# The first head pair's q and k loaded into both partition halves, and the buffers of the gated branch in another order

## The chip, the cores and the metric

The kernel runs on one core of a Trainium2 chip. The metric is the device time of one execution in microseconds (us). Before the change the median of three runs is 1768.68 us (1766.93 to 1769.41).

## The reference, cut to what matters

One step of a hybrid layer for 1024 prompt tokens and 64 decode tokens, model width 1024. One projection `h @ w_in` gives q, k, v (512 columns each, 8 heads of 64), the SSM input u and two gates of 1024 columns. Then:

```
z = (q @ k.T) / 8; log_keep = log_sigmoid(-z) where key < query
w = exp(log_sigmoid(z) + sum of log_keep over later visible keys); o_attn = w @ v
o_ssm = y * sigmoid(y @ w_glu)            # y = gelu of the S5 scan's output
merged = sigmoid(g_attn) * (o_attn @ w_branch_attn) + sigmoid(g_ssm) * (o_ssm @ w_branch_ssm)
```

After that come the output projection, a SwiGLU feed-forward layer and the per-layer embedding gate, all with RMS norms. Decode queries attend to a cache of 2048 past rows as well. The raw k and v are outputs too.

## The kernel before, in words

**Arithmetic.** All matrices are float32. For the weight products each operand is split into a rounded high part and the remainder (`split`, L124: ScalarE rounds, VectorE subtracts), and `mm3` (L133) makes three matmuls of one product: high by high, high by low, low by high. A feature-major product (`fm_iter`, L257) takes 128 output columns and goes over the 1088 tokens in three chunks of 364, 362 and 362 (`CH`); with 8 k-tiles a chunk is 24 matmuls into one PSUM bank of tag `pj`, followed by an evacuation `evac`.

**Attention operands.** For scores of a head, one matmul contracts over 128 partitions that hold q's high part in 64 of them and its low part in the other 64. The key tile `ks` holds in `[:, 0]` the high part of k in both halves and in `[:, 1]` the low part in both halves; two matmuls (L764) then give all four products. `project_pair(j)` (L621) prepares two heads. For pairs 1 to 3 it computes q, k, v from weights, chunk by chunk. For pair 0 the three column blocks were computed earlier (`rest`, L1490) and lie in the DRAM scratch `pp`; `projected` (L693) loads them. In both cases q is split into `qh` and `ql` (L633, L634), and four DMAs (L649) copy the halves into the two `qs` tiles; k is split into `kh` and `kl` (L660, L663) and eight DMAs (L677) copy them into the two `ks` tiles. The four tiles qh, ql, kh, kl share the tag `hl` with two buffers. `tok_out` (L698) transposes k and v by TensorE for the outputs; for v it also fills the `vs` tiles by GpSimd.

**The stage before attention.** `glu` (L585) loads y, splits it into `ya`, makes four sigmoid products into `sg`, multiplies by y (L605), splits the result into four `bs` tiles, and then runs eight products `w_branch_ssm` (the "branch stage"): for each m a gate tile `gl` (two buffers) is loaded from `gd` (L613), three chunks of 12 matmuls are multiplied into it (L616), and it is stored again (L618).

**What sets the order.** A queue of dense work (`rest`) holds gate columns; `fill(1)` takes its next piece. `attention` (L861) prepares pair 0, then takes `G3 = 4` pieces of the queue while `self.cut` is 0, when a piece is a whole chunk of 24 matmuls. After that it walks through the string `ORDER`, made by `order` (L52): a digit is a step of that head, `d` a decode step, `p` a step of the projections of pairs 1 to 3, `g` one piece of the queue, `E` an early load for the merge. There `CUT = 3`, and a piece is a third of a chunk. `gs` is how many `g` fall on each of the four pairs. `hold` (L151) keeps p and g pieces behind a recent score matmul. What is left of the queue is taken after attention (`fill(48)`, L1553). The framework orders every engine's instructions by a timeline that it simulates when the program is built, with program order as priority, so instructions of later code can stand before those of earlier code. All loads and stores here are issued by SyncE's queue (SP), in order.

**Memory.** Buffers of a pool get addresses by tag in the order in which tags first appear. `glu` is a left pool; attention has a left pool (`attA`) that begins at the same address, and a right pool (`att`) that grows down from the top, whose first tag is `ks` (three tiles). A tile waits for the earlier tiles whose bytes it reuses (`reuse_waits="tile"`).

Of the kernel before, what the change touches and what calls it, by code (L numbers as in the profile page):

```python
# [8 lines left out]
F32 = mybir.dt.float32  # L9
F32R = mybir.dt.float32r  # L10
BF = mybir.dt.bfloat16
AF = mybir.ActivationFunctionType
OP = mybir.AluOpType
# [4 lines left out]
SEQ = 1024  # L18
DEC = 64
TOK = SEQ + DEC  # L20
PAST = 2048
HD = 64
# [7 lines left out]
CHU = ((0, 368), (368, 360), (728, 360))  # L30
LVL = 3
G1, G2 = 5, 4
G3 = 4
CUT = 3
NC = 3
HP = 5
# [15 lines left out]
def order(L, steps, d0, d1, p0, p1, gs, e):  # L52

    ev = []
    for x in range(8):
        ev += [(x + L * f, 0, str(x)) for f in steps]
    for j in range(4):
        ev += [(2 * j + d0 + (d1 - d0) * k / 5, 1, "d") for k in range(5)]
        if j < 3:
            ev += [(2 * j + p0 + (p1 - p0) * k / (9 * NC), 2, "p") for k in range(9 * NC + 1)]  # L60
        ev += [(2 * j + 2 * (k + .5) / gs[j], 3, "g") for k in range(gs[j])]
    ev.append((e, 4, "E"))
    return "".join(x[2] for x in sorted(ev))


ORDER = order(L=1.7, steps=(0, 0.23, 0.42, 0.76), d0=-0.09, d1=1.77, p0=-0.36, p1=1.49, gs=(9, 15, 3, 21), e=7)


class Net:
# [515 lines left out]
    def glu(self, P):  # L585

        nc = self.nc
        Y, YA, B = [None] * 4, [None] * 4, []
        for k in (0, 2, 1, 3):
            y = P.tile([128, T, NCH], F32, name="y", tag="y", bufs=4)  # L590
            nc.sync.dma_start(y, self.ydr[k * 128:(k + 1) * 128])
            ya = P.tile([128, 2, TOK], F32R, name="ya", tag="ya", bufs=4)
            for c0, n0, n in ((0, 0, SEQ // T), (SEQ, S0, DEC // T)):
                h, l = (ya[:, i, c0:c0 + n * T].rearrange("p (c t) -> p t c", t=T) for i in range(2))
                self.split(h, l, y[:, :, n0:n0 + n])
            Y[k], YA[k] = y, ya
        for m in range(4):
            s = P.tile([128, TOK], F32, name="sg", tag="sg", bufs=2)

            def evac(ci, c0, n, ps, s=s):  # L600
                nc.scalar.activation(s[:, c0:c0 + n], ps, AF.Sigmoid)
            self.fm_cols(self.I["w_glu"][0], m * 128, 4, evac, acts=YA)
            for c0, n0, n in ((0, 0, SEQ // T), (SEQ, S0, DEC // T)):
                v = s[:, c0:c0 + n * T].rearrange("p (c t) -> p t c", t=T)
                nc.vector.tensor_mul(v, v, Y[m][:, :, n0:n0 + n])  # L605
            if "o_ssm" in self.dbg:
                nc.sync.dma_start(self.dbg["o_ssm"][m * 128:(m + 1) * 128], s)
            b = P.tile([128, 2, TOK], F32R, name="bs", tag="bs", bufs=4)
            self.split(b[:, 0], b[:, 1], s)
            B.append(b)  # L610
        for m in range(8):
            g = P.tile([128, TOK], F32, name="gl", tag="gl", bufs=2)
            nc.sync.dma_start(g, self.gd[8 + m])  # L613

            def evac(ci, c0, n, ps, g=g):
                nc.vector.tensor_mul(g[:, c0:c0 + n], ps, g[:, c0:c0 + n])  # L616
            self.fm_cols(self.I["w_branch_ssm"][0], m * 128, 4, evac, acts=B)
            nc.sync.dma_start(self.gd[8 + m], g)  # L618


    def project_pair(self, PB, PA, j, out):  # L621

        nc, P = self.nc, PA
        PJ = PB if j % 2 else PA
        w_in = self.I["w_in"][0]
        qh = P.tile([128, SEQ], F32R, "qh", "hl")
        ql = P.tile([128, SEQ], F32R, "ql", "hl")
        qb = PJ.tile([128, 128], F32, "qb", f"qb{j % 2}")
        nc.gpsimd.memset(qb, 0.0)

        def evac_q(ci, c0, n, ps):
            m = min(n, SEQ - c0)
            nc.scalar.activation(qh[:, c0:c0 + m], ps[:, :m], AF.Copy, scale=0.125)  # L633
            nc.vector.scalar_tensor_tensor(ql[:, c0:c0 + m], ps[:, :m], 0.125, qh[:, c0:c0 + m],  # L634
                                           op0=OP.mult, op1=OP.subtract)
            if m < n:
                for h in range(2):
                    hs = slice(h * 64, (h + 1) * 64)
                    nc.scalar.activation(qb[hs, hs], ps[hs, m:n], AF.Copy, scale=0.125)
        if j:  # L640
            yield from self.fm_iter(w_in, j * 128, 8, evac_q)
        else:
            x = self.projected(PB.tile([128, 2, SEQ], F32R, "ks", "ks").bitcast(F32).rearrange("p a b -> p (a b)")[:, :TOK], 0)
            for ci, (c0, n) in enumerate(CH):
                evac_q(ci, c0, n, x[:, c0:c0 + n])
        Q = [PJ.tile([128, SEQ], F32R, "qs", f"qs{j % 2}") for h in range(2)]
        for h in range(2):
            for i in range(2):
                nc.sync.dma_start(Q[h][i * 64:(i + 1) * 64].bitcast(F32),  # L649
                                  (qh, ql)[i][h * 64:(h + 1) * 64].bitcast(F32))  # L650
        kt = P.tile([128, TOK], F32, "kT", "raw")
        if not j:
            self.projected(kt, 1)
        kn = PJ.tile([128, DEC], F32, "kn", f"kn{j % 2}")
        kh = P.tile([128, SEQ], F32R, "kh", "hl")
        kl = P.tile([128, SEQ], F32R, "kl", "hl")

        def evac_k(ci, c0, n, ps):
            m = min(n, SEQ - c0)
            nc.scalar.activation(kh[:, c0:c0 + m], ps[:, :m], AF.Copy)  # L660
            if j:
                nc.scalar.activation(kt[:, c0:c0 + n], ps, AF.Copy)
            nc.vector.tensor_sub(kl[:, c0:c0 + m], ps[:, :m], kh[:, c0:c0 + m])  # L663
            if m < n:
                nc.vector.tensor_copy(kn, ps[:, m:n])
        if j:
            yield from self.fm_iter(w_in, SBW + j * 128, 8, evac_k)
        else:
            for ci, (c0, n) in enumerate(CH):
                evac_k(ci, c0, n, kt[:, c0:c0 + n])  # L670
        self.tok_out(P, kt, 2, 6, j, None)
        K = []
        for h in range(2):
            ks = PB.tile([128, 2, SEQ], F32R, "ks", "ks")
            for i in range(2):
                for r in range(2):
                    nc.sync.dma_start(ks[i * 64:(i + 1) * 64, r].bitcast(F32),  # L677
                                      (kh, kl)[r][h * 64:(h + 1) * 64].bitcast(F32))
            K.append(ks)
        vt = P.tile([128, TOK], F32, "vT", "raw")  # L680

        def evac_v(ci, c0, n, ps):
            nc.scalar.activation(vt[:, c0:c0 + n], ps, AF.Copy)
        if j:
            yield from self.fm_iter(w_in, 2 * SBW + j * 128, 8, evac_v)
        else:
            self.projected(vt, 2)
        V = [PJ.tile([128, 8, 2, HD], F32R, "vs", f"vs{j % 2}") for _ in range(2)]
        vn = PJ.tile([DEC, 128], F32, "vn", f"vn{j % 2}")
        self.tok_out(P, vt, 3, 7, j, (V, vn))  # L690
        out[j] = list(zip(Q, K, V)), (kn, qb, vn)

    def projected(self, x, i):  # L693
# [167 lines left out]
    def attention(self, P, PA, fill, early):  # L861

        self.oad = [self.dram.tile([128, TOK], F32, name=f"oad{j}") for j in range(4)]
        ops, self.miles = {}, []
        pa = PA.__enter__()
        for _ in self.project_pair(P, pa, 0, ops):
            pass
        self.cut = 0
        for _ in range(G3):
            fill(1)  # L870
        def projections():
            for j in range(1, 4):
                yield from self.project_pair(P, pa, j, ops)
                yield

        def decodes():
            for j in range(4):
                yield from self.decode(P, j, *ops[j][1])

        live = {"p": projections(), "d": decodes()}  # L880
        self.cut = CUT
        for c in ORDER:
            if c == "E":
                PA.__exit__(None, None, None)
                early()
            elif c == "g":
                with self.hold(HG):
                    fill(1)
            elif c == "p":
                with self.hold(HP):  # L890
                    next(live[c], None)
            else:
                if c not in live:
                    j, h = divmod(int(c), 2)
                    live[c] = self.head(P, j, h, *ops[j][0][h])
                next(live[c], None)
        for c in "01234567d":
            for _ in live[c]:
                pass
        self.cut = 0  # L900
# [710 lines left out]
```

## Time and profile before

| | |
|---|---|
| median of three runs | 1768.68 us |
| the profiled execution | 1768.44 us, span from first to last instruction 1766.7 us |
| TensorE busy | 1692.9 us (96%) |
| VectorE, ScalarE, GpSimd busy | 1041.0 (59%), 731.2 (41%), 522.3 (30%) us |
| mean granted TensorE clock | 0.985 of full |

Rows of `windows` views give, for a stretch, its length, the busy time of TensorE, its weight loads, VectorE, ScalarE and GpSimd, each with its number of instructions, then the granted clock (1.00 is 2.4 GHz, 0.50 is 1.2 GHz), the mean busy share of the DMA engines and GB/s. Rows of a `timeline` give start, duration, engine, line, operation, output<-input; brackets hold the idle time before it and what ended it. Rows of groups end with busy time, mean ns of one, idle time before.

### The profile page before, as it was taken

How to read it: one execution, taken by the hardware profiler on the slowest of the kernel's cores; microseconds unless marked ns; L12 is line 12 of the kernel's file. 1: busy time of each engine (PE TensorE's matmuls, PEld its weight loads, DVE VectorE, ACT ScalarE, POOL GpSimd, SP SyncE). 2: the span in 40 equal slices, each digit the busy share in tenths (PEclk: the TensorE clock that was granted, in tenths of full speed). 3: DMA queues.
4: the chain of work that ended last, by engine and by line, in shares of the span. 5: the costliest groups of instructions: out<-in, count | busy, mean ns of one | idle time of the engine just before them, and what ended most of it. 6: DMA issues, size and time to landing. Idle time of an engine off the chain costs nothing.

```text
span 1766.7 us, 24728 instructions
## 1 busy us (share of the span) xinstructions
PE 1692.9 (96%) x9092; PEld 1478.4 (84%) x9092; DVE 1041.0 (59%) x1579; ACT 731.2 (41%) x1355; POOL 522.3 (30%) x450
## 2 busy tenths in 40 slices
PE   8999999989999888899997999999999999999998
PEld 6999999989898877798786788888888877888886
DVE  7437917337768777866464656555555455445674
ACT  6431135135545556533343333333333344444542
POOL 2026200022313233233330544446444213001453
PEclk9999999999999999999998999999999999999999
DMA  8352563874344332157445354445444386665332
GB/s 287 93 148 64 125 148 116 260 187 121 87 107 105 90 98 84 48 174 231 138 154 182 124 154 127 153 138 184 154 139 141 113 303 203 203 190 168 104 111 89
DMA packets 220841, 258.23 MB, mean 146 GB/s; under 512 B 26272, under 2 KB 168720, under 8 KB 220704
## 3 DMA queue, kind: packets, MB, share of 16 engines
q1 hardware_dynamic: 220064, 255.21, 47.8%
q0 software_dynamic: 656, 1.44, 0.6%
q8 instruction: 72, 1.18, 0.3%
q14 instruction: 49, 0.40, 0.1%
HBM read 165.32 MB, written 76.51 MB: 137 GB/s over the span
## 4 chain that ended last, share of the span: by engine, by line
PE 72%; DVE 13%; DMA 6%; ACT 3%; issue 3%; POOL 1%; SPq 1%; DVEq 0%; POOLq 0%; ACTq 0%
PE pj L1205 13%; PE tr L1205 6%; PE pj L137 6%; PE pj L139 6%; PE pj L138 6%; PE z L1371 3%; DVE p L735 3%; PE z L1205 3%; PE pj L1371 3%; PE tr L1371 2%; PE av L811 2%; PE z L138 2%; PE z L139 2%; PE z L137 2%; PE tr L781 1%
## 5 line engine op out<-in xcount | busy, mean ns | idle before, releaser
L137 PE MATMUL pj<-H,wh 128*128 128x362 f32 (+3 forms) x648 | 218.1, 337 | 5.9 <-DVE ql L634 3.7
L139 PE MATMUL pj<-H,wl 128*128 128x362 f32 (+3 forms) x648 | 215.4, 333 | 0.6 <-DVE wl L115 0.6
L138 PE MATMUL pj<-H,wh 128*128 128x362 f32 (+3 forms) x648 | 214.7, 332 | 0.0
L126 DVE TENSOR_TENSOR wl<-raw,wh 128x1024 fp32r<-128x1024 f32 x96 | 131.4, 1373 | 114.0 <-ACT wh L125 112.7
L737 POOL TENSOR_TENSOR w<-w,p 128x383 f32<-128x383 f32 (+4 forms) x68 | 92.7, 1373 | 314.4 <-DVE w L739 185.7
L125 ACT ACTIVATE wh<-raw 128x1024 fp32r<-128x1024 f32 x96 | 101.2, 1059 | 118.3 <-PE z L1371 45.5
L137 PEld LDWEIGHTS pj<-H,wh 128*128 128x128 f32 x648 | 123.0, 190 | 7.6 <-DVE ql L634 4.0
L139 PEld LDWEIGHTS pj<-H,wl 128*128 128x128 f32 x648 | 122.7, 189 | 1.5 <-DVE wl L115 1.0
L138 PEld LDWEIGHTS pj<-H,wh 128*128 128x128 f32 x648 | 123.0, 190 | 1.0 <-issue 0.4
L1205 PE MATMUL pj<-H,s 128*128 128x512 f32 x480 | 118.2, 395 | 0.0
L148 POOL TENSOR_TENSOR rs<-rs,mhalf 128x1 f32<-128x1 f32 (+1 forms) x54 | 32.6, 605 | 277.6 <-DVE rs L147 277.5
L1205 PEld LDWEIGHTS pj<-H,s 128*128 128x128 f32 x480 | 89.9, 188 | 21.0 <-DVE c L1238 0.3
L125 ACT ACTIVATE s<-st 128x512 fp32r<-128x512 f32 x80 | 50.3, 629 | 124.3 <-PE pj L1205 112.8
L1139 POOL TENSOR_TENSOR st<-raw 128x512 f32<-128x512 f32 x40 | 60.9, 1524 | 132.3 <-DVE H L126 54.0
L126 DVE TENSOR_TENSOR s<-st,s 128x512 fp32r<-128x512 f32 x80 | 68.1, 852 | 39.2 <-ACT s L125 38.5
L119 ACT ACTIVATE wh<-raw 128x1024 fp32r<-128x1024 f32 (+1 forms) x52 | 46.6, 898 | 99.7 <-PE av L138 52.1
L115 DVE TENSOR_TENSOR wl<-raw,wh 128x1024 fp32r<-128x1024 f32 (+1 forms) x50 | 51.1, 1022 | 57.7 <-ACT wh L119 57.6
L786 DVE TENSOR_TENSOR wtl<-tr,wth 128x512 fp32r<-128x512 f32 (+2 forms) x112 | 55.2, 496 | 50.5 <-ACT wth L785 50.0
L785 ACT ACTIVATE wth<-tr 128x512 fp32r<-128x512 f32 (+2 forms) x112 | 50.3, 453 | 83.3 <-PE tr L781 42.1
L733 ACT ACTIVATE p<-z 128x512 f32<-128x512 f32 (+4 forms) x116 | 59.0, 509 | 42.6 <-PE z L835 16.7
L735 DVE TENSOR_TENSOR_SCAN p<-p,zero 128x384 f32<-128x384 f32 (+4 forms) x68 | 73.9, 1094 | 0.2
L1205 PE MATMUL pj<-H,wh 128*128 128x512 f32 x224 | 72.5, 401 | 0.6 <-ACT H L125 0.4
(553 smaller groups left out, 4634.0 us busy)
## 6 DMA issues: line engine op xcount, KB each, us to landing
sd<-c SPq DMA_DIRECT2D x77, 256.0 KB, 3.2
raw<-sd SPq DMA_DIRECT2D x77, 256.0 KB, 2.8
raw<-in_w_in_dram SPq DMA_DIRECT2D x32, 512.0 KB, 5.5
raw<-in_w_ffn_gate_dram SPq DMA_DIRECT2D x22, 512.0 KB, 3.7
raw<-in_w_ffn_up_dram SPq DMA_DIRECT2D x22, 512.0 KB, 4.7
wd<-in_w_ffn_down_dram SPq DMA_DIRECT2D x44, 256.0 KB, 3.4
td<-wd SPq DMA_DIRECT2D x22, 512.0 KB, 3.2
raw<-td SPq DMA_DIRECT2D x44, 256.0 KB, 3.0
```

What stands on the lines that cost most here:

```text
L125: self.nc.scalar.activation(wh, raw, AF.Copy)
L126: self.nc.vector.tensor_sub(wl, raw, wh)
L137: self.nc.tensor.matmul(out, wh, xh, start=i == 0, stop=False)
L138: self.nc.tensor.matmul(out, wh, xl, start=False, stop=False)
L139: self.nc.tensor.matmul(out, wl, xh, start=False, stop=i == n - 1)
L733: nc.scalar.activation(p, z, AF.Sigmoid, scale=-1.0)
L735: nc.vector.tensor_tensor_scan(p[:, ::-1], p[:, ::-1], self.zero.to_broadcast([128, n]), 1.0 if carry is None else carry, op0=OP.mult, op1 ...
L737: (nc.gpsimd if e == 'g' else nc.vector).tensor_tensor(w[:, :n - 1], w[:, :n - 1], p[:, 1:], op=OP.mult)
L786: nc.vector.tensor_sub(wl[:, a:b], ps[:, a:b], wh[:, a:b])
L1139: op(t, x, y)
L1205: self.nc.tensor.matmul(out, a[i][:, k], b[j][:, k], start=start and k == i == j == 0, stop=stop and k == 3 and i == 1, skip_group_check=n ...
L1371: nc.tensor.matmul(B[b + n], x[:, 0, c], y[:, 1], start=new and p == j == 0, stop=p == 10 and j == 2, skip_group_check=not new)
```

## The change

For pair 0 a new function `first_pair` replaces `project_pair`. It loads each head's 64 rows of q twice, into both halves of the partitions, and of k likewise, straight into the final tiles. ScalarE rounds all 128 rows of q; VectorE overwrites the second half with the remainder. k is split in place. The staging tiles of tag `hl` and the twelve copies between SBUF tiles are not used for pair 0. In `glu` the tiles `ya`, `bs` and the first two `gl` are allocated ahead of `y` and `sg`. `G3` goes from 4 to 0 and `gs[0]` from 9 to 13.

```diff
-G3 = 4
+G3 = 0
-ORDER = order(L=1.7, ..., gs=(9, 15, 3, 21), e=7)
+ORDER = order(L=1.7, ..., gs=(13, 15, 3, 21), e=7)
 def glu(self, P):
-        Y, YA, B = [None] * 4, [None] * 4, []
+        Y = [None] * 4
+        YA, B = ([P.tile([128, 2, TOK], F32R, name=n, tag=n, bufs=4) for _ in range(4)] for n in ("ya", "bs"))
+        GL = [P.tile([128, TOK], F32, name="gl", tag="gl", bufs=2) for m in range(2)]
...
-            g = P.tile([128, TOK], F32, name="gl", tag="gl", bufs=2)
+            g = GL[m] if m < 2 else P.tile([128, TOK], F32, name="gl", tag="gl", bufs=2)
...
+    def first_pair(self, PB, PA, out):
+        nc = self.nc
+        Q = [PA.tile([128, SEQ], F32R, "qs", "qs0") for h in range(2)]
+        x = PB.tile([128, 2, SEQ], F32R, "ks", "ks").bitcast(F32)
+        K = [PB.tile([128, 2, SEQ], F32R, "ks", "ks") for h in range(2)]
...
+        for h in range(2):
+            rows = slice(h * 64, h * 64 + 64)
+            for i in range(2):
+                nc.sync.dma_start(x[i * 64:i * 64 + 64, h], self.pp[0][rows, :SEQ])
+            for i in range(2):
+                nc.sync.dma_start(K[h][i * 64:i * 64 + 64, 1].bitcast(F32), self.pp[1][rows, :SEQ])
+            nc.scalar.activation(Q[h], x[:, h], AF.Copy, scale=0.125)
+            nc.vector.scalar_tensor_tensor(Q[h][64:], x[64:, h], 0.125, Q[h][64:], op0=OP.mult, op1=OP.subtract)
+            raw = K[h][:, 1].bitcast(F32)
+            self.split(K[h][:, 0], K[h][:, 1], raw)
+        nc.sync.dma_start(qn, self.pp[0][:, SEQ:])
+        nc.sync.dma_start(kn, self.pp[1][:, SEQ:])
...
+        kt = self.projected(PA.tile([128, TOK], F32, "kT", "raw"), 1)
+        self.tok_out(PA, kt, 2, 6, 0, None)
+        vt = self.projected(PA.tile([128, TOK], F32, "vT", "raw"), 2)
+        V, vn = self.values(PA, PA, 0, vt)
...
-        for _ in self.project_pair(P, pa, 0, ops):
-            pass
+        self.first_pair(P, pa, ops)
```

`values` holds the three lines that allocated V and vn and called `tok_out` for v. The branches of `project_pair` for pair 0 are deleted.

## Rows read from the trace of the kernel before

**Rows 1.** The page, busy time and instructions of each engine.
```profile
PE 1692.9 (96%) x9092; PEld 1478.4 (84%) x9092; DVE 1041.0 (59%) x1579; ACT 731.2 (41%) x1355; POOL 522.3 (30%) x450
```

**Rows 2.** Windows by stage, from the branch stage's end to attention's end.
```profile
344.00:360.00 16.00, 16.00 (x101) 15.92 (x100) 5.24 (x9) 4.45 (x10) 0.00 (x0) 1.00 0.92 272
360.00:380.00 20.00, 15.83 (x90) 15.04 (x89) 5.61 (x13) 3.65 (x13) 3.94 (x9) 0.91 0.89 224
...
400.00:480.00 80.00, 77.36 (x506) 70.36 (x505) 56.78 (x108) 42.80 (x102) 22.46 (x23) 1.00 0.44 110
...
572.00:752.00 180.00, 157.53 (x961) 138.56 (x960) 137.56 (x241) 103.14 (x237) 52.02 (x42) 0.93 0.31 81
```

**Rows 3.** Waits of TensorE between 344 and 400 us: total, times, longest.
```profile
PE pj L137 <- DVE ql L634: 3.5, 1, 3.5
PE pj L137 <- ACT gs L914: 0.7, 1, 0.7
```

**Rows 4.** Timeline of TensorE around the longer wait.
```profile
369.33 0.49 PE L764 MATMUL z<-ks,qs 128*128 128x128 f32 x2
...
373.76 0.43 PE L137 MATMUL pj<-H,wh 128*128 128x362 f32 x1 [3.52 <-DVE ql L634]
...
377.10 0.51 PE L138 MATMUL pj<-H,wh 128*128 128x362 f32 x1
```

**Rows 5.** Timelines of ScalarE and VectorE, the instructions that the wait was for.
```profile
371.94 0.84 ACT L633 ACTIVATE qh<-pj 128x364 fp32r<-128x364 f32 x2 [9.82 <-DMA ks<-kh]
...
373.17 0.98 DVE L634 SCALAR_TENSOR_TENSOR ql<-pj,qh 128x364 fp32r<-128x364 f32 x2 [10.40 <-ACT w L734]
```

**Rows 6.** Timeline of SP's queue, loads and copies of pair 0.
```profile
346.16 0.53 SPq L695 DMA_DIRECT2D ks<-pp  x1
...
348.42 0.38 SPq L824 DMA_DIRECT2D kr<-in_cache_k_dram  x1
...
367.98 0.62 SPq L677 DMA_DIRECT2D ks<-kl  x1
368.70 1.19 SPq L695 DMA_DIRECT2D vT<-pp  x1
```

**Rows 7.** Windows of 4 us in the same stretch.
```profile
368.00:372.00 4.00, 2.25 (x16) 1.94 (x14) 0.00 (x0) 0.06 (x1) 0.00 (x0) 1.00 1.03 205
372.00:376.00 4.00, 2.24 (x11) 1.92 (x12) 2.32 (x5) 1.67 (x6) 0.62 (x1) 0.84 0.97 307
376.00:380.00 4.00, 4.00 (x21) 4.00 (x20) 1.39 (x2) 0.00 (x0) 3.03 (x7) 0.73 0.66 186
```

**Rows 8.** Timeline of VectorE from the sigmoid products into the branch stage.
```profile
296.96 2.47 DVE L605 TENSOR_TENSOR sg<-sg,y 128x1024 f32<-128x1024 f32 x2
300.67 1.29 DVE L126 TENSOR_TENSOR bs<-sg,bs 128x1088 fp32r<-128x1088 f32 x1 [1.24 <-ACT bs L125]
...
307.61 0.54 DVE L616 TENSOR_TENSOR gl<-pj,gl 128x362 f32<-128x362 f32 x1 [1.44 <-PE pj L139]
...
312.20 0.54 DVE L616 TENSOR_TENSOR gl<-pj,gl 128x364 f32<-128x364 f32 x1 [3.40 <-DMA gl<-gd]
```

**Rows 9.** DMA queue from 276 to 306 us, then from 304 to 346: packets, MB, share.
```profile
q1 hardware_dynamic: 2208, 1.47, 15.5%
...
q1 hardware_dynamic: 7212, 10.33, 78.0%
```

**Rows 10.** The page, groups of whole-tile splits.
```profile
L126 DVE TENSOR_TENSOR wl<-raw,wh 128x1024 fp32r<-128x1024 f32 x96 | 131.4, 1373 | 114.0 <-ACT wh L125 112.7
L125 ACT ACTIVATE wh<-raw 128x1024 fp32r<-128x1024 f32 x96 | 101.2, 1059 | 118.3 <-PE z L1371 45.5
```

**Rows 11.** Windows of 4 us at one dip of the clock late in attention.
```profile
636.00:640.00 4.00, 1.46 (x9) 1.07 (x9) 3.96 (x8) 1.46 (x4) 0.86 (x1) 1.00 0.92 224
640.00:644.00 4.00, 2.47 (x10) 2.17 (x11) 2.44 (x5) 0.90 (x3) 0.00 (x0) 0.62 0.31 101
644.00:648.00 4.00, 4.00 (x21) 3.68 (x21) 2.17 (x4) 1.51 (x5) 0.00 (x0) 0.52 0.02 4
```

More of the change, by code (lines that the diff above doesn't have):

```diff
@@ L63, in order @@
     return "".join(x[2] for x in sorted(ev))
-ORDER = order(L=1.7, steps=(0, 0.23, 0.42, 0.76), d0=-0.09, d1=1.77, p0=-0.36, p1=1.49, gs=(9, 15, 3, 21), e=7)
+ORDER = order(L=1.7, steps=(0, 0.23, 0.42, 0.76), d0=-0.09, d1=1.77, p0=-0.36, p1=1.49, gs=(13, 15, 3, 21), e=7)
 class Net:
@@ L591, in glu @@
             nc.sync.dma_start(y, self.ydr[k * 128:(k + 1) * 128])
-            ya = P.tile([128, 2, TOK], F32R, name="ya", tag="ya", bufs=4)
+            ya = YA[k]
             for c0, n0, n in ((0, 0, SEQ // T), (SEQ, S0, DEC // T)):
@@ L595, in glu @@
                 self.split(h, l, y[:, :, n0:n0 + n])
-            Y[k], YA[k] = y, ya
+            Y[k] = y
         for m in range(4):
@@ L607, in glu @@
                 nc.sync.dma_start(self.dbg["o_ssm"][m * 128:(m + 1) * 128], s)
-            b = P.tile([128, 2, TOK], F32R, name="bs", tag="bs", bufs=4)
-            self.split(b[:, 0], b[:, 1], s)
-            B.append(b)
+            self.split(B[m][:, 0], B[m][:, 1], s)
         for m in range(8):
-            g = P.tile([128, TOK], F32, name="gl", tag="gl", bufs=2)
+            g = GL[m] if m < 2 else P.tile([128, TOK], F32, name="gl", tag="gl", bufs=2)
             nc.sync.dma_start(g, self.gd[8 + m])
@@ L618, in glu, with values @@
             nc.sync.dma_start(self.gd[8 + m], g)
+    def values(self, P, PJ, j, vt):
+        V = [PJ.tile([128, 8, 2, HD], F32R, "vs", f"vs{j % 2}") for _ in range(2)]
+        vn = PJ.tile([DEC, 128], F32, "vn", f"vn{j % 2}")
+        self.tok_out(P, vt, 3, 7, j, (V, vn))
+        return V, vn
+    def first_pair(self, PB, PA, out):
[3 more added lines that the diff above has]
+        K = [PB.tile([128, 2, SEQ], F32R, "ks", "ks") for h in range(2)]
+        qb = PA.tile([128, 128], F32, "qb", "qb0")
+        nc.gpsimd.memset(qb, 0.0)
+        kn = PA.tile([128, DEC], F32, "kn", "kn0")
+        qn = PB.tile([128, DEC], F32, "od", "od")
+        for h in range(2):
[10 more added lines that the diff above has]
+        nc.sync.dma_start(kn, self.pp[1][:, SEQ:])
+        for h in range(2):
+            hs = slice(h * 64, (h + 1) * 64)
+            nc.scalar.activation(qb[hs, hs], qn[hs], AF.Copy, scale=0.125)
+        kt = self.projected(PA.tile([128, TOK], F32, "kT", "raw"), 1)
+        self.tok_out(PA, kt, 2, 6, 0, None)
+        vt = self.projected(PA.tile([128, TOK], F32, "vT", "raw"), 2)
+        V, vn = self.values(PA, PA, 0, vt)
+        out[0] = list(zip(Q, K, V)), (kn, qb, vn)
     def project_pair(self, PB, PA, j, out):
@@ L639, in evac_q @@
                     nc.scalar.activation(qb[hs, hs], ps[hs, m:n], AF.Copy, scale=0.125)
[L640 to L645, printed above, removed]
+        yield from self.fm_iter(w_in, j * 128, 8, evac_q)
         Q = [PJ.tile([128, SEQ], F32R, "qs", f"qs{j % 2}") for h in range(2)]
@@ L651, in project_pair @@
         kt = P.tile([128, TOK], F32, "kT", "raw")
-        if not j:
-            self.projected(kt, 1)
         kn = PJ.tile([128, DEC], F32, "kn", f"kn{j % 2}")
@@ L660, in evac_k @@
             nc.scalar.activation(kh[:, c0:c0 + m], ps[:, :m], AF.Copy)
-            if j:
-                nc.scalar.activation(kt[:, c0:c0 + n], ps, AF.Copy)
+            nc.scalar.activation(kt[:, c0:c0 + n], ps, AF.Copy)
             nc.vector.tensor_sub(kl[:, c0:c0 + m], ps[:, :m], kh[:, c0:c0 + m])
@@ L665, in evac_k @@
                 nc.vector.tensor_copy(kn, ps[:, m:n])
[L666 to L670, printed above, removed]
+        yield from self.fm_iter(w_in, SBW + j * 128, 8, evac_k)
         self.tok_out(P, kt, 2, 6, j, None)
@@ L683, in evac_v @@
             nc.scalar.activation(vt[:, c0:c0 + n], ps, AF.Copy)
[L684 to L690, printed above, removed]
+        yield from self.fm_iter(w_in, 2 * SBW + j * 128, 8, evac_v)
+        V, vn = self.values(P, PJ, j, vt)
         out[j] = list(zip(Q, K, V)), (kn, qb, vn)
```

## The prediction, made before the changed kernel was run

> **What bounds the kernel now.** I read the page's busy times first: TensorE is busy 1692.9 us, 96% of the span [rows 1], so a change pays only where it removes TensorE's idle time, its matmuls at the lower clock, or its work. The next view is the busy time by stage [rows 2]. The reader is to see three things. From 344 to 360 us TensorE has no gap: it works through the four gate chunks of G3 (16.00 us of 16.00, so 4 us a chunk of 24 matmuls). From 360 to 380 it is busy 15.83 of 20 us, and the granted clock is 0.91. From 572 to 752 it is idle for 180 − 157.5 = 22.5 us at a mean clock of 0.93, the largest loss in attention.
>
> The third view is what TensorE waited for between 344 and 400 us: 3.5 us on ql (L634), 0.7 us on the evacuation L914 [rows 3]. The fourth follows the 3.5 us back. TensorE stops after the first score matmuls, which began at 369.33, and goes on at 373.76 with a projection chunk of pair 1 [rows 4]. Its PSUM bank had to be evacuated by qh and ql. ScalarE's qh had sat 9.82 us until a DMA ks<-kh had landed, and VectorE's ql came behind it [rows 5]: qh of pair 1 takes over an `hl` buffer, and the tag's two buffers still hold pair 0's kh and kl until the copies into `ks` have read them. Those copies end late because the last are issued up to 367.98, at the end of a queue that began with the load of q at 346.16 [rows 6]. After the stop the clock falls: 0.84 and 0.73 in two windows of 4 us [rows 7], with matmuls of 362 columns at 0.51 us [rows 4].
>
> **The change part by part.** The sum is made against the profiled execution, 1768.44 us, which lies 0.24 us under the median; its span is 1766.7 us.
>
> *TensorE's work.* The transposes, projections and gate chunks are the same in number: 0.
>
> *The staging of pair 0.* Removed: 12 copies between tiles, 3 qh, 3 ql, 3 kh, 3 kl and one kn. Pair 1's qh then finds both `hl` buffers unused, so the wait of rows 3 has no cause left: 3.5 us, and the smaller wait of 0.7 us in the same crowd of evacuations, together −4.2 us. What is late next is qh's reuse by k of pair 1, three chunks (12 us) later and without a wait in this trace. The fall of the clock goes with the stop: (1 − 0.84) × 4 + (1 − 0.73) × 4 = 0.64 + 1.08 = −1.7 us [rows 7].
>
> *Where the loads go.* Today the load of q stands behind the whole branch stage (346.16 [rows 6]), since `ks`, at the top of the right pool, lies on the last `bs` and `gl`, which the stage reads to its end. In the new order `ya` is lowest, under `attA`, and `y` and `sg` are highest, under `ks`. Their last readers are L605 (from 296.96) and the last split of sg (300.67 + 1.29 = 302.0) [rows 8]. So x, K and kT can be loaded from about 302 us, 40 us before attention begins. The four chunks of G3 are then not needed as cover.
>
> *What this costs in the branch stage.* Eight loads of 256 KB, one of 544 KB and two small ones are 2.7 MB. The queue is nearly empty from 276 to 306 (15.5%) and 78.0% busy from 304 to 346, where it moves 10.33 MB [rows 9]: 10.33 MB / (0.780 × 42 us) = 315 GB/s while busy, and 0.22 × 42 = 9.2 us free. At 315 GB/s the loads take 8.6 us and fit. The other end is the 205 GB/s at which DMAs, mostly copies into 64 partitions, filled the queue at 368 to 372 [rows 7]: 13.3 us, 4.1 us too many. A late `gl` reaches TensorE only after a while: the second m's last chunk ends when its multiply starts, at 307.61, so the third m's first ends about 309.6 (2 us a chunk of 12 matmuls), and its multiply waits for `gl` until 312.20 [rows 8], and with four PSUM banks in turn the bank is wanted again three chunks later, at 315.6; it is free at 312.7, so 2.9 us are spare. I take +1 us, near the first end because half of it fits ahead of 304, and keep 0 to +6 (4.1 and a fall of the clock of 1.7).
>
> The Trainium skill, "DMA: Bandwidth & Descriptors", section "Rules for kernel authors", speaks against such loads: two transfers to the two halves of the partitions serialise on the same engines, and one transfer over 128 should be used. "SBUF — State Buffer", section "Door 1", gives 196 GB/s for 64 partitions at 1 MiB, which fits the 205 GB/s of rows 7. An estimate by that figure is 2.1 MB / 196 = 10.7 us for the eight, 12.4 us with kT, 3.2 us over the free time, and a total near 1765.
>
> *The splits.* ScalarE rounds four tiles of 128 by 1024 (4 × 1.06 us), VectorE makes two remainders of k at 1.37 us [rows 10] and two of q on 64 partitions, at most as long. VectorE has three multiplies of 0.54 us [rows 8] and a weight split per 6 us there, and one such instruction ahead of a multiply is less than the 2.9 us spare: 0, and up to +1.5 if two come together.
>
> *The queue.* The 24 chunks left before attention are taken as 4 in G3, 48 / 3 = 16 in attention and 4 behind it; afterwards 52 / 3 = 17.3 in attention and 6.7 behind it. The 1.3 chunks go to pair 0, where TensorE idles 2.64 us of 80 [rows 2]: I take −1 us, between 0 and −2.6. The 2.7 chunks behind attention are work that moves, TensorE being full there: 0.
>
> *V of pair 0.* It is loaded after k's transposes, at 368.70 today [rows 6]; it may come at about 346, and projections of pair 1 lie beside it: 0.
>
> Sum: −4.2 − 1.7 + 1 − 1 = −5.9 us. 1768.44 − 5.9 = 1762.5, and 0.24 more for the median: 1762.8 us. Its own range is 1760 (no stall in the branch stage, all of pair 0's idle filled) to 1767.
>
> **The rivals.**
>
> *The branch stage pays.* The loads delay `gl`, TensorE stalls by 6 us, and the waits only move forward: 1762.8 − 1 + 6 = 1768. For it speaks that the multiply already waits 3.40 us for `gl` [rows 8]; against it the empty queue before 304.
>
> *The loads don't come early.* If `ks` still lies on live bytes, or the planner issues the loads late, k is ready some 13 us after 343 (5 to 8 us of DMA, four splits). The projections of pair 1 cover that, but a stop like that of rows 3 can come back: 1767 to 1769. Against it: loads do pass earlier code in this queue, as that of kr for a decode step at 348.42, ahead of copies that the code issues before it [rows 6].
>
> *Attention's late half gets worse (slower).* The timeline is planned anew, and fixed orders of engines shift against the chip's times. One dip of the late half, as at 636 to 648 us, costs 2.54 + 1.53 us idle and (0.38 + 0.48) × 4 = 3.4 us of clock, 7.5 us [rows 11]. One more leaves +1.6 us (1770.3), two more make it 1778. It decides from the second dip on. For it: 22.5 us are idle there, so the balance is delicate [rows 2]. Against it: heads and pieces per pair are unchanged there (15, 3, 21).
>
> *The late half gets better.* One dip fewer: 1755.
>
> **How the numbers follow.** Forecast 0.52, branch stage 0.15, loads not early 0.08, late half worse 0.15, late half better 0.10. A measurement tells about 0.2%, 3.5 us, from no change. Faster: nearly nine tenths of the first case, all of the last and a little of the second, 0.58. Slower: most of the late half worse and some mishap of the second, 0.16. The rest, 0.26, within. The range that leaves out the ends of the two cases of the late half is 1755 to 1772.
>
> **What would show it.** Right: no load of pair 0 behind 320 us, no DMA ks<-kh of pair 0, first scores of head 0 near 355 instead of 369.33, no wait of TensorE above 1 us on L634 and clock 1.00 in the 40 us after the branch stage. The stage's price shows as idle time before its matmuls of bs. Wrong: TensorE idle between 304 and 344 by more than 3 us, or its idle time between the start of pair 2's heads and the merge away from 22.5 us by more than 5 us.

## The result: slower by 0.94%

The changed kernel takes 1784.94 us (median of 5 runs, 1779.01 to 1789.40) against 1767.95 us for the kernel before beside it; the ratio is 1.0094, with a 95% interval of 1.0075 to 1.0112. The forecast was 1762.8 us and its range ended at 1772. The profiled execution is the fastest of the five (1779.01 us, span 1777.2 us, mean granted clock 0.985); the others had 0.978 to 0.983, so the trace shows about 10.5 of the 17 us. Where the other 6 lie no trace shows.

TensorE's line on the page, which answers to [rows 1], shows the same number of instructions and 2.3 us more busy time:

```profile
PE 1695.2 (95%) x9092; PEld 1477.6 (83%) x9092; DVE 1040.8 (59%) x1576; ACT 733.5 (41%) x1353; POOL 519.4 (29%) x450
```

Windows of the changed kernel over the stretch where attention begins, in the columns of [rows 2]:

```profile
344.00:360.00 16.00, 13.57 (x82) 13.00 (x80) 5.25 (x6) 5.57 (x9) 0.00 (x0) 1.00 0.95 240
360.00:380.00 20.00, 15.87 (x91) 14.33 (x92) 9.00 (x20) 6.45 (x19) 5.14 (x10) 0.89 0.67 174
380.00:400.00 20.00, 15.53 (x72) 12.25 (x71) 7.20 (x13) 6.30 (x14) 4.43 (x2) 0.77 0.14 41
```

TensorE is now idle 56 − 44.97 = 11.0 us between 344 and 400, and the clock takes (1 − 0.89) × 20 + (1 − 0.77) × 20 = 6.8 us more: 17.8 us. Before, the same sums over windows of 4 us are 4.8 and 1.7 us [rows 2, 7]. The difference, 11.3 us, is as large as that of the two spans, 10.5 us. From 572 to 760 us idle time and clock cost 39.0 us against 35.1 before; other stretches give 5 us back.

TensorE's five longest waits between 340 and 400 us, where [rows 3] show two waits of together 4.2 us:

```profile
PE tr L865 <- POOL w L758: 3.3, 1, 3.3
PE tr L726 <- DMA vT<-pp: 2.2, 1, 2.2
PE pj L137 <- DVE ql L672: 1.6, 1, 1.6
PE pj L137 <- ACT qb L677: 1.2, 1, 1.2
PE z L856 <- issue: 0.8, 1, 0.8
```

The wait on ql is still there, now with another cause. SP's queue, which answers to [rows 6]:

```profile
342.00 0.32 SPq L618 DMA_DIRECT2D gd<-gl  x1
343.61 0.38 SPq L106 DMA_DIRECT2D raw<-in_w_in_dram  x1
344.05 1.23 SPq L641 DMA_DIRECT2D ks<-pp  x2
345.59 1.08 SPq L643 DMA_DIRECT2D ks<-pp  x2
...
352.95 0.32 SPq L716 DMA_DIRECT2D kT<-pp  x1
...
368.35 0.69 SPq L716 DMA_DIRECT2D vT<-pp  x1
```

The first load of q is issued at 344.05, behind the last store of the branch stage (342.00), and not at 302. In the line of ScalarE the first rounding of q (L644) waits for it, ahead of an evacuation of pair 1 (L671):

```profile
345.44 0.47 ACT L671 ACTIVATE qh<-pj 128x364 fp32r<-128x364 f32 x1 [3.11 <-PE pj L139]
351.94 1.06 ACT L644 ACTIVATE qs<-ks 128x1024 fp32r<-128x1024 f32 x1 [6.04 <-DMA ks<-pp]
352.91 0.45 ACT L671 ACTIVATE qh<-pj 128x362 fp32r<-128x362 f32 x1
354.09 1.06 ACT L125 ACTIVATE ks<-ks 128x1024 fp32r<-128x1024 f32 x1 [0.72 <-DMA ks<-pp]
...
358.41 1.06 ACT L125 ACTIVATE ks<-ks 128x1024 fp32r<-128x1024 f32 x1 [1.18 <-DMA ks<-pp]
```

VectorE's line is held up in the same way: the remainder of q (L645) stands ahead of the remainder `ql` of pair 1 (L672).

```profile
353.04 1.22 DVE L645 SCALAR_TENSOR_TENSOR qs<-ks,qs 64x1024 fp32r<-64x1024 f32 x1 [6.56 <-ACT qs L644]
354.29 0.54 DVE L672 SCALAR_TENSOR_TENSOR ql<-pj,qh 128x362 fp32r<-128x362 f32 x1
```

So the projections that should have covered the loads fill two PSUM banks, and for a while nobody empties them: the second chunk ends at 349.35 (349.02 + 0.33), and its evacuation starts at 352.91. TensorE stops:

```profile
349.02 0.33 PE L139 MATMUL pj<-H,wl 128*128 128x362 f32 x1
...
354.88 0.43 PE L137 MATMUL pj<-H,wh 128*128 128x364 f32 x1 [1.60 <-DVE ql L672]
...
360.25 0.42 PE L785 MATMUL z<-ks,qs 128*128 128x128 f32 x2
...
373.71 1.07 PE L726 MATMUL tr<-ident,vT 128*128 128x128 f32 x8 [2.20 <-DMA vT<-pp]
...
390.58 1.11 PE L865 MATMUL tr<-ident,w 128*128 128x128 f32 x4 [3.32 <-POOL w L758]
```

This stop is 1.6 us of the 11.0 us idle; the rest comes after it. The first scores start at 360.25, 9 us earlier than in [rows 4], but what follows has too little beside it: v's transposes wait for vT, and the transposes of a decode step wait for a product on GpSimd with no other matmul in line. After each of the last two stops the clock is at 1.2 GHz for a while:

```profile
372.00:376.00 4.00, 1.55 (x10) 1.12 (x11) 1.51 (x4) 0.56 (x3) 0.83 (x3) 0.95 0.24 91
376.00:380.00 4.00, 4.00 (x16) 3.44 (x16) 2.01 (x6) 1.66 (x5) 3.45 (x6) 0.50 0.55 144
...
388.00:392.00 4.00, 1.27 (x5) 0.87 (x5) 2.96 (x3) 0.88 (x3) 3.79 (x2) 0.66 0.08 16
392.00:396.00 4.00, 3.67 (x15) 2.97 (x15) 0.44 (x2) 0.98 (x3) 0.00 (x0) 0.50 0.06 19
```

### The profile page after: what moved, and what is told of

The parts are those of the page before. It is cut to its first block, busy times and chain, and to the rows that moved or that the text cites. A ratio compares the mean times of both kernels' runs of the same rounds, so it can differ in the third digit from the quotient of the medians.

```text
span 1777.2 us, 24735 instructions
## 1 busy us (share of the span) xinstructions
PE 1695.2 (95%) x9092; PEld 1477.6 (83%) x9092; DVE 1040.8 (59%) x1576; ACT 733.5 (41%) x1353; POOL 519.4 (29%) x450
## 4 chain that ended last, share of the span: by engine, by line
PE 74%; DVE 12%; DMA 6%; ACT 3%; issue 3%; POOL 1%; SPq 1%; DVEq 0%; POOLq 0%; ACTq 0%
PE pj L1225 13%; PE tr L1225 6%; PE pj L137 6%; PE pj L138 6%; PE pj L139 6%; PE z L1391 3%; PE z L1225 3%; DVE p L756 3%; PE pj L1391 3%; PE tr L1391 2%; PE z L138 2%; PE z L139 2%; PE z L137 2%; PE av L832 2%; PE av L1391 1%
```

## The experiments

The first theory after the result: the loads start near 344 us in either kernel, and the change took away the 16 us of gate chunks that stood beside them (cover). Rivals: the new staging is itself slow; the new buffer order delays the loads. Ratios are to the kernel before on the same chip, with 95% intervals.

**Cover given back.**

```diff
-G3 = 0
+G3 = 4
-gs=(13, 15, 3, 21)
+gs=(9, 15, 3, 21)
```

> The changed kernel with G3 = 4 and gs[0] = 9 again; first_pair and the new buffer order stay. Cover theory (the loss is the 16 us of gate chunks that no longer stand beside pair 0's loads, which begin near 344 us in either kernel): TensorE's idle time between 344 and 400 us falls from about 11 us to under 5 and the time to 1762 to 1769, faster than or equal to before. Staging theory (eight loads into half the partitions ahead of kT and vT are themselves slower): still 1774 or more. Layout theory (ks lies on bs now, so the loads wait for the branch stage): still 1774 or more.

Measured: 1765.62 us, 0.9986 (0.9975 to 0.9997). Its windows:

```profile
344.00:360.00 16.00, 15.51 (x94) 15.21 (x93) 3.31 (x5) 2.96 (x4) 0.20 (x1) 1.00 0.91 256
360.00:380.00 20.00, 17.33 (x111) 16.51 (x111) 10.44 (x17) 7.53 (x16) 0.83 (x3) 1.00 0.71 200
380.00:400.00 20.00, 19.38 (x120) 17.68 (x118) 9.44 (x17) 9.16 (x22) 8.61 (x10) 1.00 0.55 133
```

Idle 3.8 us and no fall of the clock, against 11.0 and 6.8. Staging and layout theories fall: both edits are still in this kernel, and it is slightly faster than before. What is left of the idle time is mostly one wait, for the block of q for the decode step (`qb`, L652), which ScalarE makes from the last of the loads:

```profile
PE z L856 <- ACT qb L652: 2.6, 1, 2.6
```

**Cover taken away from the old staging** (the kernel before with G3 = 0 and gs[0] = 13).

> The kernel before with only G3 = 0 and gs[0] = 13; old staging through qh, ql, kh, kl and old buffer order. Cover theory: slower, at least as slow as the changed kernel, 1780 to 1795, since the old chain from the load of q to the last copy into ks is longer. Staging and layout theories: 1764 to 1770, as before.

Measured: 1786.18 us, 1.0107 (1.0094 to 1.0120). TensorE's longest waits:

```profile
PE z L764 <- DMA ks<-kh: 9.9, 1, 9.9
PE pj L137 <- DVE ql L634: 3.3, 1, 3.3
PE z L764 <- DMA ks<-kl: 2.7, 1, 2.7
PE tr L705 <- DMA kT<-pp: 2.4, 1, 2.4
```

The same two schedule numbers cost the old staging as much. TensorE's waits for the copies that first_pair removes are 12.6 us here; in [rows 3], with the cover, there is none. The loads and splits ahead of the copies are part of these 12.6 us.

**The old buffer order in the changed kernel**, and **the new buffer order alone in the kernel before**. The edit in both is the glu function of the other kernel.

> The changed kernel with the buffer order of the gated branch as before (ks lies on ya and sg, dead since 302 us); first_pair, G3 = 0 and gs[0] = 13 stay. Cover theory: the first load still stands at about 344 us in SP's queue, behind the last store of gl, so the time stays at 1779 to 1790. Layout theory: the loads start by 310 us and the time falls to 1768 or less.

> The kernel before with only the new buffer order of the gated branch. Cover and staging theories: 1766 to 1770, no change. Layout theory: slower than 1774, because ks lies on bs.

Measured: 1778.98 us, 1.0067 (1.0052 to 1.0081), and 1768.03 us, 1.0001 (0.9991 to 1.0011). Alone the order does nothing. In the addresses of the built program the right pool grows upward from its first tag: `ks` lay on `ya` and `sg` before, and the change puts it on `bs`, the opposite of what I had read out of the code. Yet with the old order the first load comes no earlier:

```profile
345.28 1.18 SPq L641 DMA_DIRECT2D ks<-pp  x2
346.75 1.08 SPq L643 DMA_DIRECT2D ks<-pp  x2
```

So the bytes are not what holds it. In all twelve kernels here that do not move the loads ahead of the branch stage, the first load of pair 0's rows is issued 1.6 to 2.3 us after that stage's last store. Whether the difference between 1.0067 and 1.0094 is the buffer order is open: the intervals overlap, and the two were not run side by side. In the profiles it lies late: between 344 and 400 us idle time and clock cost 18.0 us here against 17.8, between 572 and 760 us 33.1 against 39.0.

**No loads of q and k.** The splits read tiles of H instead, so pair 0's attention is over other numbers.

```diff
-            for i in range(2):
-                nc.sync.dma_start(x[i * 64:i * 64 + 64, h], self.pp[0][rows, :SEQ])
-            for i in range(2):
-                nc.sync.dma_start(K[h][i * 64:i * 64 + 64, 1].bitcast(F32), self.pp[1][rows, :SEQ])
+            x, raw = (self.H[:, 2 * i + h, 0, :SEQ].bitcast(F32) for i in range(2))
```

> The changed kernel without the eight loads of q and k of pair 0: the splits read tiles of H that lie in SBUF, so the attention of pair 0 is over other numbers; kT, vT and the two small loads stay, G3 = 0 and gs[0] = 13 stay. Lateness theory (TensorE loses because q and k arrive 8 to 15 us after the branch stage and ScalarE and VectorE stand in line behind them): the time falls to 1770 or less and TensorE's idle time from 344 to 400 us to under 6 us. Thin-fill theory (even with q and k at hand the first decode and head steps wait on each other and on v, and pair 0 lacks matmuls to lay beside them): 1774 or more, with the waits at 372 to 396 us as in the changed kernel.

Measured: 1770.09 us, 1.0016 (1.0003 to 1.0030). Of the 0.94% about 0.78 are gone with the eight loads. In the profiled execution (1775.03 us, 5 us above the median) the idle time from 344 to 400 us is 6.0 us and the clock costs 0.06 × 56 = 3.4:

```profile
344.00:400.00 56.00, 50.03 (x296) 45.62 (x295) 31.44 (x54) 24.16 (x58) 13.27 (x15) 0.94 0.45 120
```

That is the lateness theory nearly to its numbers; a rest remains, part of it a wait for kT (1.8 us). Without the eight loads the later ones come earlier as well, so this run does not part a late q and k from a late kT and vT.

**Half the cover** (G3 = 2, gs[0] = 11).

> The changed kernel with G3 = 2 and gs[0] = 11: 8 us of cover. Lateness theory: the loads then trail by about 8 us less, half of the loss is gone, 1770 to 1776. If the loss comes from the plan as a whole and not from the length of the cover, no such order: anywhere from 1762 to 1785.

Measured: 1771.60 us, 1.0025 (1.0009 to 1.0040). With 0, 2 and 4 chunks: 1.0094, 1.0025, 0.9986. The loss falls with the length of the cover; the pieces of pair 0 go along (13, 11, 9), and the next two runs part the two.

**Cover with 13 pieces for pair 0** (G3 = 4, gs[0] = 13), and **no cover with 9** (G3 = 0, gs[0] = 9).

> The changed kernel with G3 = 4 and gs[0] = 13 kept, so 1.3 chunks move from behind attention into pair 0. Lateness theory: as with gs[0] = 9, 1762 to 1768, since the pieces of ORDER are not what costs. If the four more pieces of pair 0 cost time: above 1771.

> The changed kernel with gs[0] = 9 and G3 = 0 left: the four chunks of the cover move behind attention whole, the fourth corner beside cover 4 with 9 and 13 pieces and cover 0 with 13. If the four more pieces of pair 0 cost by themselves what they cost with the cover (0.43%, 7.6 us), 1776 to 1780. If the missing cover alone is the loss and the pieces help a pair 0 that lacks matmuls, 1784 or more.

Measured: 1772.62 us, 1.0029 (1.0013 to 1.0044), and 1780.70 us, 1.0076 (1.0059 to 1.0093). The cover is worth 0.90% with 9 pieces and 0.65% with 13. So the cover is the larger part of the loss at either number of pieces. The lateness theory missed the first run: with the cover there, four more pieces in pair 0 cost 0.43%, where I had expected no loss. The second run fell between its two expectations: without the cover the four pieces make 0.18%, which the intervals do not tell from nothing. In the profile of the first the loss lies late: between 572 and 760 idle time and clock cost 39.2 us (35.1 with 9 pieces), and TensorE idles 4.6 us from 760 to 900 (0.8 with 9 pieces). There 24 − 4 − 52/3 = 2.7 chunks are left to stand behind attention where there were 4. That this is the cause was not tried.

**Only the staging changed** (first_pair, old buffer order, G3 = 4, gs[0] = 9).

> first_pair with G3 = 4 and gs[0] = 9 and the old buffer order: only the staging is changed. If the new buffer order costs some us (it puts ks on bs): 1758 to 1764. If it does not: 1762 to 1768, as with the new order.

Measured: 1764.41 us, 0.9978 (0.9964 to 0.9992). The same kernel with the new buffer order had 0.9986: not told apart.

**The loads really early.** To test the step that failed by itself, the gated branch's pool is parted, and the pool with `ks` opens before the branch stage.

```diff
-        with pool("glu") as P:
-            N.glu(P)
+        GB = pool("glub")
+        PG = GB.__enter__()
+        with pool("glu", "right") as P:
+            N.glu(P, PG)
+        KP = pools(tc, "ksp", dict(ks=3, od=1, raw=1), "right")
+        KP.__enter__()
+        N.first_loads(KP)
+        N.glu_branch(PG)
+        GB.__exit__(None, None, None)
```

> The changed kernel (G3 = 0, gs[0] = 13) with its loads really early: the gated branch's pool is parted in two, so that y, ya and sg close before the branch stage, and a pool with ks, od and the raw tile opens there; q, k and kT of pair 0 are loaded and k is split beside the branch stage. This is what the prediction thought the change to do. Prediction's step (loads from 302 us, a stall of 0 to 6 us in the branch stage, +1 taken): first load near 302, TensorE's idle time 304 to 344 under 2 us, 344 to 400 under 4 us, time 1760 to 1768. Rival, the loads crowd the gl ring: idle 304 to 344 of 4 us or more. Rival, pair 0 lacks matmuls beside the first decode and head steps whenever the loads come: idle 344 to 400 of 6 us or more, time 1772 or more.

> The same early loads with G3 = 4 and gs[0] = 9. If the cover is only needed because the loads are late, it is worth nothing here: within 3 us of the run without cover. If the first steps of attention need the cover anyway, 5 us or more faster than that run, 1758 to 1764.

Measured: 1773.49 us, 1.0030 (1.0016 to 1.0044) without cover, and 1766.22 us, 0.9997 (0.9985 to 1.0009) with it. SP's queue of the first of the two:

```profile
302.25 1.14 SPq L641 DMA_DIRECT2D ks<-pp  x2
...
307.96 0.38 SPq L727 DMA_DIRECT2D kT<-pp  x1
308.43 0.38 SPq L622 DMA_DIRECT2D gd<-gl  x1
...
318.13 2.33 SPq L617 DMA_DIRECT2D gl<-gd  x2
```

The loads come at 302.25, as the prediction had thought, and idle time from 344 to 400 falls to 1.0 us:

```profile
344.00:400.00 56.00, 55.01 (x348) 51.42 (x346) 31.00 (x52) 23.41 (x54) 14.00 (x16) 1.00 0.53 148
```

But they stand ahead of the first gate tile's store, and the load of the third gate tile is issued only at 318.13 (307.04 in the kernel before, whose branch stage began some 3 us earlier). That load goes into the buffer that the store reads, and the store, issued at 308.43, took 9.6 us to land. The branch stage pays. TensorE's one long wait there, and then the windows around it:

```profile
322.79 0.43 PE L137 MATMUL pj<-bs,wh 128*128 128x362 f32 x1 [4.41 <-DVE gl L620]
```

```profile
304.00:308.00 4.00, 3.91 (x24) 3.60 (x23) 3.18 (x6) 0.64 (x1) 0.00 (x0) 1.00 0.98 236
308.00:312.00 4.00, 4.00 (x26) 4.00 (x25) 2.06 (x3) 1.58 (x2) 0.00 (x0) 1.00 1.06 237
312.00:316.00 4.00, 4.00 (x26) 4.00 (x25) 1.50 (x3) 1.06 (x1) 0.00 (x0) 1.00 1.02 325
...
320.00:324.00 4.00, 1.21 (x5) 1.22 (x6) 1.64 (x4) 0.00 (x0) 0.00 (x0) 0.91 0.86 278
324.00:328.00 4.00, 4.00 (x18) 4.00 (x18) 1.07 (x2) 0.00 (x0) 0.00 (x0) 0.66 0.41 161
```

That is 4.5 us idle and (0.09 + 0.34) × 4 = 1.7 us of clock, 6.2 us. Against the kernel before, 5.5 us are won between 344 and 400 us (6.5 to 1.0) and 6.2 lost here. The run with cover is 0.33% faster than the one without, and its median 7.3 us lower, so by the expectation the cover is needed for more than late loads; its time still missed the expected 1758 to 1764, and it pays in the branch stage too (4.3 us idle and 1.7 of clock). Between 400 and 572 us TensorE idles 8.7 us without the cover and 4.9 with it. But the two runs differ in the pieces of pair 0 as well (13 and 9), which alone made 0.43% above. There the pieces cost between 572 and 900 us and not here (5.3 us idle between 400 and 572 with cover and 13 pieces), which speaks for the cover; no run parts the two with early loads.

**The small loads first.**

```diff
+        nc.sync.dma_start(qn, self.pp[0][:, SEQ:])
+        nc.sync.dma_start(kn, self.pp[1][:, SEQ:])
+        for h in range(2):
+            hs = slice(h * 64, (h + 1) * 64)
+            nc.scalar.activation(qb[hs, hs], qn[hs], AF.Copy, scale=0.125)
         for h in range(2):
             rows = slice(h * 64, h * 64 + 64)
```

> first_pair with G3 = 4, gs[0] = 9 and the old buffer order, and the two small loads with the block for the decode step moved ahead of the eight large ones. There TensorE waits 2.3 us for qb (L652), made from the last of the loads, and the clock falls after it. If that wait costs what it shows, it goes and the time falls by 2 to 4 us, to 1760 to 1763. If another wait takes its place: 1764 as without the move.

Measured: 1762.75 us, 0.9974 (0.9958 to 0.9989). The wait on qb is gone from the trace, and between 344 and 400 the clock stays at 2.4 GHz; two shorter waits are left there:

```profile
PE tr L726 <- DMA kT<-pp: 0.7, 1, 0.7
PE tr L802 <- POOL w L758: 0.6, 1, 0.6
```

In time it is not told apart from 0.9978 without the move. Its median is the lowest here, below the kernel before and the changed one: the staging of the change, without its other two edits.

## Why the prediction was wrong, point by point

*Where the loads go: the step that failed.* The prediction said that in the new order `ks` lies under `y` and `sg`, "so x, K and kT can be loaded from about 302 us" and "the four chunks of G3 are then not needed as cover". The first half was wrong. `ks` lies on `bs`; and the buffer order doesn't set the time of the load, since with either order it stands at 344 to 345 us in queues without cover. The reason given for 346.16 in the kernel before, that `ks` lies on the last `bs` and `gl`, is wrong as well: there it lay on `ya` and `sg`. What moved the loads was opening the pool and issuing them ahead of the branch stage: together these brought the first to 302.25. Which of the two counts was not tried. The second half fails with the first: taking the cover away cost 0.65 to 0.90%, and with the loads early the kernel without cover was still 0.33% slower than the one with it. The row that I used as support, a load that passed earlier copies [rows 6], passes within one pool and says nothing on passing the end of another.

*The wait that goes, −4.2 and −1.7 us.* Its cause went, as said, but pair 1's banks now wait because the lines of ScalarE and VectorE wait for the load of q. The prediction looked for the next late thing at k of pair 1 and not at what stands ahead of the evacuations in that line. With the cover it came out at less than half: idle and clock from 344 to 400 fall from 6.5 to 3.8 us in the first experiment, 2.7 us of the 5.9. The clock's 1.7 us went whole; of the idle time only 1.0 us, since the wait for `qb`, 2.6 us, took the place of the wait on ql.

*The rival "the loads don't come early"* had the right event and got 0.08. Its price, 1767 to 1769, was at least 16 us too low. It let pair 1's projections cover the loads; they did so only until two banks were full (353.3), since their evacuations need ScalarE and VectorE, which were waiting. It also had no term for what comes behind the first scores, the waits for vT and for GpSimd's product and the fall of the clock after each.

*The branch stage, +1 us, 0 to +6.* Measured where the loads are early: 6.2 us, just past the far end. While the loads into half the partitions ran, the queue was full at 236 to 237 GB/s, near the 205 of [rows 7] and not the 315 that I leaned to. The Trainium skill, "DMA: Bandwidth & Descriptors", section "Rules for kernel authors", holds that transfers to the two halves serialise; the windows agree, with 325 GB/s once they had passed. So does the kernel before, which loads q and k of pair 0 once, into 128 partitions: from 348 to 352 us it moves 373 GB/s and the changed kernel 245, with the engines as full in both (DMA share 1.04). How far the rate, and how far the loads' place ahead of the gate tile's store, made the 6.2 us was not tried. The estimate of 3.2 us from the 196 GB/s that the Trainium skill, "SBUF — State Buffer", section "Door 1", gives lay closer than my +1.

*Pieces in pair 0, −1 us, and the chunks behind attention, 0.* With the cover, 13 pieces instead of 9 cost 0.43%. The prediction counted the idle time that they could fill and put the chunks that leave the end at nothing; the profile of that run has the loss between 572 and 900 us, and its cause stays open.

*Attention's late half.* 39.0 us of idle time and clock against 35.1 in the profiles: half a dip. It is the smaller part of the loss: with the old buffer order these stretches cost 33.1 us, and the kernel was still 0.67% slower.

## What to carry to other kernels

Before dropping filler work, find in the trace what runs beside it and ask whether the filler's replacement can run while the load is late: here it stopped once its evacuations stood in ScalarE's and VectorE's lines behind the instructions that waited for the load. Don't read a planner's freedom out of buffer addresses; look for a load in the trace that crossed the same boundary. And test a staging change apart from the schedule change that it is meant to allow: here the first alone gained 0.2% and the second alone lost 1.1%.

## What the runs showed that was not expected

A stop of TensorE can cost more than its length: in the changed kernel stops of 2.2 and 3.3 us (up to 373.7 and 390.6 us) were each followed by a window of 4 us wholly at 1.2 GHz, and the clock's part from 344 to 400 (6.8 us) is more than half of the idle time (11.0 us). Not every stop does: in the first experiment the wait of 2.6 us for `qb` left TensorE 1.40 us of work in 4, and the clock stayed at 2.4 GHz:

```profile
364.00:368.00 4.00, 1.40 (x14) 1.35 (x13) 2.69 (x3) 2.85 (x6) 0.00 (x0) 1.00 0.88 266
368.00:372.00 4.00, 3.93 (x25) 3.55 (x24) 2.70 (x6) 1.06 (x6) 0.70 (x2) 1.00 0.51 149
```

What tells the two cases apart no run here shows.
